# A bidirectional SSD scan with its step sizes moved into the exponent, and low weight parts made by DMA from an earlier point on

## The chip, the cores and the metric

One core of one Trainium2 chip runs the whole program. The engines named below are TensorE (PE in the profile, PEld for its weight loads), VectorE (DVE), ScalarE (ACT), GpSimd (POOL) and SyncE (SP, which issues most loads). The metric is the device time of one execution in microseconds, the median of several runs.

## The reference

One encoder layer runs on two independent sequences, a prompt of 512 tokens and a sample of 1024, with the same float32 weights. What matters here:

```python
u = group_rmsnorm(h, norm_mix_pre)
proj = u @ w_in                       # z, x/B/C, dt, and three hyena streams
# SSD: chunks of 128 tokens, 16 heads in 2 groups, forward and backward
a = dt * a_h;  a_cs = jnp.cumsum(a, axis=2)
decay_ts = jnp.exp(jnp.where(causal, seg, -jnp.inf))     # seg = a_cs[t] - a_cs[s]
scores = jnp.einsum('bctgn,bcsgn->bcgts', cr, br)
y_diag = jnp.einsum('bcgrts,bcsgrp->bctgrp', scores[:, :, :, None] * decay_ts, x * dt)
y_ssd = y_fwd + y_bwd + xs * ssd_d    # then gate with silu(z) and group norm
# hyena: short convolutions, then a long convolution by FFT
mix = concat([y_ssd, y_hy]) @ w_out   # residual, SwiGLU FFN, gated embedding
```

Inside a chunk, each pair of tokens (t, s) gets the score C_t.B_s times a decay of head and direction times the step size dt_s. On the diagonal both directions contribute with decay 1.

## The kernel before, in words

Matrix products keep nearly full float32 accuracy by splitting each operand into a high part (rounded to the fp32r format) and a low part (what the rounding lost), and running three matmuls: high x high (L301), low x high (L302), high x low (L303). A streamed weight half-tile of 128x512 is loaded by SyncE into `wst`. ScalarE then writes the high part `whi` (L292), and GpSimd subtracts it from the weight to get the low part `wlo` (L293). That is `split_w`. In `split_dma` ScalarE writes minus the rounded weight into `wlo` (L284), a DMA issued by GpSimd adds the weight to it (L285), and ScalarE writes `whi` in a second pass (L286). The flag `self.dma_lo` chooses between them in `load_w`. Six buffers of each of `wst`, `whi` and `wlo` run ahead of TensorE.

`build` calls the stages in this order: projections of the prompt, filters, scan of the prompt (`ssd(P)`), hyena projections and long convolution of the prompt; then for the sample the z and x/B/C projections, `ssd(S)`, `project_hy(S)` (the second convolution projections), `longconv(S)`; then the prompt's output projection, embedding projection and FFN, and the sample's. The order of the code isn't the order of execution: the Tile framework schedules all instructions with a timeline of its own and writes one in-order queue per engine, so a stage that keeps VectorE busy has large matrix products of a later stage between its instructions on TensorE. In the schedule before, `project_hy(S)` accompanies the prompt's long convolution and the start of the sample's scan, the prompt's output and embedding projections accompany the rest of that scan, and the prompt's FFN accompanies the sample's long convolution.

The scan handles one chunk c and one group g (8 heads) at a time: 8 units for the prompt, 16 for the sample, three pipeline stages. `stage_a` loads the cumulative decays of both directions, broadcast over the partitions, into `rw`, and computes the scores (L607), masked for the two directions into `su` and `sl` (L609, L610). For each head VectorE takes the smaller of the two directions' exponents (L615) and ScalarE the exponential (L617); that is E. Also for each head, ScalarE scales `sl` with the backward dt (L618) and VectorE adds `su` times the forward dt (L619); that is W. One VectorE product per unit multiplies W into E (L621). `stage_b` multiplies by x on TensorE (L628), adds D times x (GpSimd, L631) and the contributions of the carried states (L645, L646), and gates with z (L647). `stage_c` transposes and stores. Once per group a backward pass over all chunks (L590 to L597) prepares the backward states.

After the output projection of the prompt has been added up (L1108), `post_steps` scales, adds the residual and normalises four tiles of 128 tokens (L1059, L1060, L333), transposes them and splits them (L326). Only then can the prompt's FFN start.

## Time and profile before

| | before |
|---|---|
| median of 3 runs | 2855.22 us (2851.17 to 2855.67) |
| profiled execution: time | 2852.23 us |
| its span | 2850.3 us |
| TensorE / VectorE / ScalarE / GpSimd busy | 94% / 61% / 47% / 48% |
| scan of the prompt | about 480 to 640 us |
| scan of the sample | about 895 to 1235 us |
| long convolution of the sample | about 1250 to 1650 us |

An engine's busy share is a mean over stages with different limits. What a change is worth has to be read in the stage it lies in, from what TensorE waits for there. A group's row gives the line, engine, operation, tiles (written<-read), shape and count, then busy us and mean ns, then the idle time just before those instructions and what ended it.

### The profile page before, as it was taken

The numbers are of one execution on the slowest core, as the hardware profiler recorded it, in microseconds if no ns is written. First come the engines' busy times: TensorE is split into PE (matmuls) and PEld (weight loads), VectorE is DVE, ScalarE is ACT, GpSimd is POOL, SyncE is SP. The second block draws the span as 40 slices with busy tenths as digits, with TensorE's granted clock in tenths as the row PEclk, the third lists the DMA queues.
The fourth block names the chain that finished last, engine by engine and source line by source line (L and its number), as shares of the span: only waits on it lengthen the run. The fifth ranks groups of instructions, "written<-read, shape, count | busy, mean of one in ns | idle before, by whom it ended". The sixth has DMA issues, their size and how long they took to land.

```text
span 2850.3 us, 41685 instructions
## 1 busy us (share of the span) xinstructions
PE 2683.8 (94%) x14696; PEld 2254.9 (79%) x14696; DVE 1742.6 (61%) x2893; ACT 1336.4 (47%) x2580; POOL 1380.7 (48%) x1137
## 2 busy tenths in 40 slices
PE   7999999999999989889999998987799999999998
PEld 5987888778888767578778776766699999877776
DVE  6767896977666896966676734475343444325345
ACT  4434445773234564745444454365533333344453
POOL 4445555443453556535444444554454444445464
PEclk9999999999999999989999999999999999999999
DMA  5544555744345576778888886565632222366665
GB/s 169 180 137 127 150 174 185 219 141 138 99 123 160 154 249 202 223 206 206 199 181 204 187 218 218 177 222 183 157 100 82 79 75 86 119 207 207 203 202 186
DMA packets 448507, 480.04 MB, mean 168 GB/s; under 512 B 29409, under 2 KB 330281, under 8 KB 445995
## 3 DMA queue, kind: packets, MB, share of 16 engines
q1 hardware_dynamic: 340923, 347.34, 40.0%
q0 software_dynamic: 28224, 68.17, 10.8%
q10 hardware_dynamic: 79152, 61.88, 6.9%
q8 instruction: 116, 1.90, 0.3%
q14 instruction: 92, 0.75, 0.1%
HBM read 346.54 MB, written 91.95 MB: 154 GB/s over the span
## 4 chain that ended last, share of the span: by engine, by line
PE 66%; DVE 15%; DMA 8%; issue 5%; POOL 3%; ACT 2%; SPq 0%; POOLq 0%; ACTq 0%; DVEq 0%
PE g L301 17%; PE g L303 16%; PE g L302 16%; PE a L302 3%; PE a L303 3%; PE a L301 3%; PE a L700 1%; DVE b L692 1%; DVE W L619 1%; DVE E L615 1%; PE a L973 1%; POOL wlo L293 1%; DMA wlo<-wst 1%; PE a L404 1%; DMA mx<-mix_s 1%
## 5 line engine op out<-in xcount | busy, mean ns | idle before, releaser
L293 POOL TENSOR_TENSOR wlo<-wst,whi 128x512 fp32r<-128x512 f32 (+1 forms) x544 | 786.1, 1452 | 756.6 <-ACT whi L292 691.5
L292 ACT ACTIVATE whi<-wst 128x512 fp32r<-128x512 f32 (+1 forms) x544 | 339.5, 628 | 532.9 <-PE g L302 330.0
L301 PE MATMUL g<-uh,whi 128*128 128x512 f32 (+1 forms) x1232 | 493.5, 401 | 8.5 <-DVE cv L393 4.4
L303 PE MATMUL g<-uh,wlo 128*128 128x512 f32 (+1 forms) x1232 | 491.6, 399 | 0.0
L302 PE MATMUL g<-ul,whi 128*128 128x512 f32 (+1 forms) x1232 | 490.9, 398 | 0.0
L301 PE MATMUL g<-bh,whi 128*128 128x256 f32 x1056 | 293.0, 283 | 14.3 <-ACT sc L1266 3.8
L303 PE MATMUL g<-bh,wlo 128*128 128x256 f32 x1056 | 294.0, 281 | 4.2 <-DMA wlo<-mx 2.7
L302 PE MATMUL g<-bl,whi 128*128 128x256 f32 x1056 | 294.3, 280 | 0.0
L301 PEld LDWEIGHTS g<-uh,whi 128*128 128x128 f32 x1232 | 233.2, 189 | 67.5 <-issue 10.4
L303 PEld LDWEIGHTS g<-uh,wlo 128*128 128x128 f32 x1232 | 232.6, 189 | 53.9 <-issue 5.8
L302 PEld LDWEIGHTS g<-ul,whi 128*128 128x128 f32 x1232 | 232.9, 189 | 53.4 <-issue 7.2
L326 DVE TENSOR_TENSOR ml<-mx,mh 128x512 fp32r<-128x512 f32 x152 | 122.4, 808 | 222.0 <-ACT mh L325 221.9
L285 POOL DMA_DIRECT2D wlo<-wst x144 | 126.0, 930 | 226.2 <-ACT wlo L284 211.1
L393 DVE SCALAR_TENSOR_TENSOR cv<-g,cols,cv 128x510 f32<-128x510 f32 (+3 forms) x192 | 193.0, 1006 | 64.9 <-ACT cv L387 62.8
L301 PEld LDWEIGHTS g<-bh,whi 128*128 128x128 f32 x1056 | 197.2, 189 | 20.0 <-DVE gt L1227 6.1
L303 PEld LDWEIGHTS g<-bh,wlo 128*128 128x128 f32 x1056 | 199.6, 189 | 4.9 <-DMA wlo<-mx 2.9
L302 PEld LDWEIGHTS g<-bl,whi 128*128 128x128 f32 x1056 | 199.5, 189 | 0.1
L301 PE MATMUL g<-whi,mh 128*128 128x512 f32 x412 | 169.7, 412 | 23.7 <-ACT mh L325 16.3
L302 PE MATMUL g<-wlo,uh 128*128 128x264 f32 (+1 forms) x576 | 191.3, 332 | 0.5 <-POOL wlo L293 0.5
L303 PE MATMUL g<-whi,ul 128*128 128x264 f32 (+1 forms) x576 | 189.9, 331 | 1.6 <-DVE rs_t L308 1.6
L309 POOL TENSOR_TENSOR rs_t<-rs_t,nhalf 128x1 f32<-128x1 f32 (+2 forms) x112 | 120.0, 1074 | 144.0 <-DVE rs_t L308 141.5
L301 PE MATMUL g<-whi,uh 128*128 128x264 f32 (+1 forms) x576 | 189.0, 330 | 0.0
(334 smaller groups left out, 6030.5 us busy)
## 6 DMA issues: line engine op xcount, KB each, us to landing
wst<-in_w_in SPq DMA_DIRECT2D x192, 256.0 KB
wlo<-wst POOLq DMA_DIRECT2D x144, 256.0 KB, 4.9
wst<-in_w_down SPq DMA_DIRECT2D x132, 256.0 KB
wst<-in_w_out SPq DMA_DIRECT2D x96, 256.0 KB
wst<-in_w_gate SPq DMA_DIRECT2D x92, 256.0 KB
wst<-in_w_up SPq DMA_DIRECT2D x92, 256.0 KB
mx<-hid_s SPq DMA_DIRECT2D x88, 256.0 KB
rw<-rows_s SPq DMA_DIRECT2D x32, 512.0 KB
```

The source lines that it names most:

```text
L285: nc.gpsimd.dma_start(lo, w, accum_op=ALU.add)
L292: nc.scalar.activation(hi, w, AF.Copy)
L293: (eng or nc.gpsimd).tensor_tensor(out=lo, in0=w, in1=hi.bitcast(F32), op=ALU.subtract)
L301: nc.tensor.matmul(ps, lh, rh, start=first, stop=False, skip_group_check=shared)
L302: nc.tensor.matmul(ps, lh, rl, start=False, stop=False, skip_group_check=shared)
L303: nc.tensor.matmul(ps, ll, rh, start=False, stop=last, skip_group_check=shared)
L309: nc.gpsimd.tensor_tensor(out=t[:, :w], in0=t[:, :w], in1=self.nhalf[:, :w], op=ALU.pow)
L326: self.nc.vector.tensor_tensor(out=lo, in0=ps, in1=hi.bitcast(F32), op=ALU.subtract)
L393: nc.vector.scalar_tensor_tensor(out[:, a:b], ps[:, a + d:b + d], wcol(w), out[:, a:b], ALU.mult, ALU.add)
L404: nc.tensor.transpose(ps[:, j * 128:(j + 1) * 128], srcs[i + j], self.ident)
L615: nc.vector.scalar_tensor_tensor(E[:, h], rw[:, 0, h], dbf[:, c, gh:gh + 1], rw[:, 1, h], ALU.add, ALU.min)
L619: nc.vector.scalar_tensor_tensor(W[:, h], su, dt[:, c, gh:gh + 1], W[:, h], ALU.mult, ALU.add)
```

## The change: what it does

In the scan the step size dt goes into the exponent as its logarithm. `ssd_prep` computes log(max(dt, 1e-37)) - a_cs for all heads and both directions. `nb` becomes the backward part of it, and `dbf` the difference of forward and backward. E is then the decay times dt in one exponential, so the per-head W falls away (8 ScalarE and 8 VectorE instructions per unit), and all eight heads are multiplied with the unmasked scores in one product, as a broadcast. The masks move to the row tiles: two GpSimd `affine_select` instructions per unit set the excluded entries of `rw` to 1e30, so that the minimum picks the other direction. The forward direction keeps the diagonal. The backward direction's diagonal, score(t,t) times backward dt, is added to D: VectorE multiplies the scores with the identity, sums over the row and forms `cdd` for the eight heads, which takes the place of D in the GpSimd product with x. The scores are copied to SBUF by ScalarE. `rw` becomes two separate tiles from a ring of three, where before it was one double tile without a second buffer.

Apart from that, `dma_lo` is set before `project_hy(S)` and no longer before the prompt's FFN, so 84 more low parts are made by `split_dma`: 48 of `project_hy(S)`, 32 of the prompt's output projection and 4 of its embedding projection.

```diff
@@ ssd_prep
         dbf, nb = self.T(kp, [128, C, 16], "dbf"), self.T(kp, [128, C, 16], "nb")
-        nc.vector.tensor_tensor(out=dbf, in0=acs[:, :, 16:32], in1=acs[:, :, 0:16], op=ALU.subtract)
-        nc.vector.tensor_scalar(nb, acs[:, :, 16:32], -1.0, None, ALU.mult)
+        nc.vector.tensor_scalar(u, dt, 1e-37, None, ALU.max)
+        nc.scalar.activation(u, u, AF.Ln)
+        nc.vector.tensor_tensor(out=u, in0=u, in1=acs, op=ALU.subtract)
+        nc.vector.tensor_tensor(out=dbf, in0=u[:, :, 0:16], in1=u[:, :, 16:32], op=ALU.subtract)
+        nc.vector.tensor_copy(nb, u[:, :, 16:32])
@@ ssd_main, stage_a
-                rw = self.T(sp, [128, 2, 8, 128], "rw")
+                rw = [self.T(sp, [128, 8, 128], "rw", bufs=3) for _ in range(2)]
                 for d in range(2):
                     nc.sync.dma_start(
-                        rw[:, d], q.rows[d, c:c + 1, g * 8:(g + 1) * 8, :].to_broadcast([128, 8, 128]))
+                        rw[d], q.rows[d, c:c + 1, g * 8:(g + 1) * 8, :].to_broadcast([128, 8, 128]))
                 xt, zt, bk, bt, ct = load(c, g, ("x", "z", "bk", "bt", "ct"))
                 ps = self.aps()
                 nc.tensor.matmul(ps[:, 0:128], bt, ct, start=True, stop=True)
-                su, sl = self.T(sp, [128, 128], "su", bufs=2), self.T(sp, [128, 128], "sl", bufs=2)
-                nc.vector.tensor_tensor(out=su, in0=ps[:, 0:128], in1=self.tri[:, 0, :], op=ALU.mult)
-                nc.vector.tensor_tensor(out=sl, in0=ps[:, 0:128], in1=self.tri[:, 1, :], op=ALU.mult)
+                cb, dg = self.T(sp, [128, 128], "su", bufs=2), self.T(sp, [128, 128], "sl", bufs=2)
+                nc.scalar.activation(cb, ps[:, 0:128], AF.Copy)
+                nc.vector.tensor_tensor(out=dg, in0=ps[:, 0:128], in1=self.ident, op=ALU.mult)
+                cd, dd = self.T(sp, [128, 1], "cd", bufs=2), self.T(sp, [128, 8], "cdd", bufs=3)
+                nc.vector.tensor_reduce(cd, dg, mybir.AxisListType.X, ALU.add)
+                hs = slice(g * 8, (g + 1) * 8)
+                nc.vector.scalar_tensor_tensor(dd, dt[:, c, 16 + g * 8:24 + g * 8], cd, self.r_D[:, hs],
+                                               ALU.mult, ALU.add)
+                big = [[0, 8], [1, 128]], [[0, 8], [-1, 128]]
+                for d in range(2):
+                    nc.gpsimd.affine_select(out=rw[d], in_=rw[d], compare_op=(ALU.is_ge, ALU.is_gt)[d],
+                                            fill=1e30, base=0, pattern=big[d], channel_multiplier=(-1, 1)[d])
                 E = self.T(sp, [128, 8, 128], "E", bufs=2)
-                W = self.T(sp, [128, 8, 128], "W")
                 for h in range(8):
                     gh = g * 8 + h
-                    nc.vector.scalar_tensor_tensor(E[:, h], rw[:, 0, h], dbf[:, c, gh:gh + 1],
-                                                   rw[:, 1, h], ALU.add, ALU.min)
+                    nc.vector.scalar_tensor_tensor(E[:, h], rw[0][:, h], dbf[:, c, gh:gh + 1],
+                                                   rw[1][:, h], ALU.add, ALU.min)
                     nc.scalar.activation(E[:, h], E[:, h], AF.Exp, bias=nb[:, c, gh:gh + 1])
-                    nc.scalar.activation(W[:, h], sl, AF.Copy, scale=dt[:, c, 16 + gh:17 + gh])
-                    nc.vector.scalar_tensor_tensor(W[:, h], su, dt[:, c, gh:gh + 1], W[:, h],
-                                                   ALU.mult, ALU.add)
-                nc.vector.tensor_tensor(out=E, in0=W, in1=E, op=ALU.mult)
-                return xt, zt, bk, ct, E
+                nc.vector.tensor_tensor(out=E, in0=E, in1=cb.rearrange("p (o t) -> p o t", o=1).to_broadcast(
+                    [128, 8, 128]), op=ALU.mult)
+                return xt, zt, bk, ct, E, dd
@@ stage_b
-                nc.gpsimd.tensor_tensor(out=h3(y), in0=h3(xt),
-                                        in1=hb(self.r_D[:, g * 8:(g + 1) * 8]), op=ALU.mult)
+                nc.gpsimd.tensor_tensor(out=h3(y), in0=h3(xt), in1=hb(dd), op=ALU.mult)
@@ build
             self.stream("m")
+            self.dma_lo = True
             self.project_hy(S, pj, us)
...
-                self.dma_lo = True
                 u, chain = self.ffn(P, 0, pl, u)
                 self.dma_lo = False
```

The schedule moves with it. On VectorE, where the norm chain of the prompt's output projection meets the last units of the sample's scan, the queue before reads from the first row scaling (L1059) on as follows. Here `acc`, `t` and `rs_t` belong to the chain, all other tiles to the scan.

```order
L1059 SCALAR_TENSOR_TENSOR acc_12614<-acc_12614,rs_t_13279,row_13268 128x1024
L645 TENSOR_TENSOR yo_9509<-a_9507,ea_8044 128x512
L609 TENSOR_TENSOR su_9546<-a_9544,tri_7985 128x128
L610 TENSOR_TENSOR sl_9547<-a_9544,tri_7985 128x128
L1059 SCALAR_TENSOR_TENSOR acc_12616<-acc_12616,rs_t_13285,row_13268 128x1024
L1060 TENSOR_TENSOR t_2592_13272<-acc_12614,t_2592_13272 128x1024
L308 TENSOR_SCALAR rs_t_13291<-ss_13288 128x1
L646 TENSOR_TENSOR y_9492<-y_9492,yo_9509 128x512
L308 TENSOR_SCALAR rs_t_13297<-ss_13294 128x1
L1060 TENSOR_TENSOR t_2593_13274<-acc_12616,t_2593_13274 128x1024
L619 SCALAR_TENSOR_TENSOR W_9551<-su_9546,dt_8015,W_9551 128x128 x3
L633 TENSOR_TENSOR y_9594<-y_9594,a_9585 128x512
```

After it (ten lines are added ahead, so L1059, L1060 and L1108 are now L1069, L1070 and L1118) the same place reads:

```order
L1069 SCALAR_TENSOR_TENSOR acc_12526<-acc_12526,rs_t_13227,row_13210 128x1024
L1070 TENSOR_TENSOR t_2640_13214<-acc_12524,t_2640_13214 128x1024
L655 TENSOR_TENSOR yo_9479<-a_9477,ea_7999 128x512
L1118 TENSOR_TENSOR acc_12525<-acc_12525,g_13049 128x512
L1118 TENSOR_TENSOR acc_12527<-acc_12527,g_13049 128x512
L1070 TENSOR_TENSOR t_2641_13216<-acc_12526,t_2641_13216 128x1024
L656 TENSOR_TENSOR y_9462<-y_9462,yo_9479 128x512
L615 TENSOR_TENSOR sl_9518<-a_9515,ident_105 128x128
L631 TENSOR_TENSOR E_9531<-E_9531,su_9517 128x1024
L308 TENSOR_SCALAR rs_t_13233<-ss_13230 128x1
L643 TENSOR_TENSOR y_9558<-y_9558,a_9549 128x512
L600 TENSOR_TENSOR pf_9561<-pf_9561,a_9564 128x512
```

The W rows are gone, and the last piece of the output projection (L1118) now stands one scan unit later relative to the scan. From it to the last low part of the FFN's input (L326) the scan has 14 rows left, and the E rows of the last unit (L628) stand ahead of it.

On GpSimd, between units of the sample's scan, the queue before reads as follows (`xw` is the state's input, `y` the unit's output, `wlo` a low weight part):

```order
L590 TENSOR_TENSOR xw_8839<-lx_8673,wd_8046 128x512
L293 TENSOR_TENSOR wlo_12665<-wst_12662,whi_12664 128x512
L631 TENSOR_TENSOR y_8733<-lx_8571,r_D_7993 128x512
L647 TENSOR_TENSOR y_8631<-y_8631,lz_8471 128x512
L309 TENSOR_TENSOR rs_t_8655<-rs_t_8655,nhalf_110 128x1
L590 TENSOR_TENSOR xw_9021<-xw_9021,wd_8046 128x512
L293 TENSOR_TENSOR wlo_12695<-wst_12692,whi_12694 128x512
L631 TENSOR_TENSOR y_8835<-lx_8673,r_D_7993 128x512
```

And in the changed kernel:

```order
L593 TENSOR_TENSOR xw_8653<-lx_8500,wd_8001 128x512
L623 AFFINE_SELECT rw_8593<-rw_8593 128x1024
L657 TENSOR_TENSOR y_8457<-y_8457,lz_8310 128x512
L642 TENSOR_TENSOR y_8553<-lx_8404,cdd_8421 128x512
L623 AFFINE_SELECT rw_8688<-rw_8688 128x1024
L309 TENSOR_TENSOR rs_t_8481<-rs_t_8481,nhalf_110 128x1
L285 DMA wlo_12571<-wst_12568 128x512
L593 TENSOR_TENSOR xw_8749<-lx_8596,wd_8001 128x512
L623 AFFINE_SELECT rw_8689<-rw_8689 128x1024
L285 DMA wlo_12578<-wst_12575 128x512
```

Two selects per unit have come in, apart from each other, and the subtractions have become DMA issues.

2 lines of the change are left out of this document (1 added, 1 removed).

## The prediction

> **What bounds the kernel now.** I read the busy shares first, then the busy time by stage, then the idle time ahead of single instructions, and last the groups on the engines that the change touches. The whole execution:
>
> ```profile
> span 2850.3 us, 41685 instructions
> PE 2683.8 (94%) x14696; PEld 2254.9 (79%) x14696; DVE 1742.6 (61%) x2893; ACT 1336.4 (47%) x2580; POOL 1380.7 (48%) x1137
> ```
>
> TensorE is busy for 94% of the span, so work taken from another engine is worth only what TensorE waits for that engine. By stage (columns: window, length, then busy us and count of PE, PEld, DVE, ACT, POOL; granted clock; DMA share; GB/s):
>
> ```profile
> 640.00:895.00 255.00, 255.00 (x1308) 214.72 (x1307) 165.82 (x228) 84.63 (x117) 107.02 (x74) 1.00 0.40 114
> 500.00:525.00 25.00, 22.44 (x101) 16.89 (x100) 20.63 (x37) 16.24 (x33) 10.45 (x8) 1.00 0.67 206
> 525.00:550.00 25.00, 23.81 (x119) 17.60 (x118) 23.96 (x50) 18.92 (x46) 10.46 (x9) 1.00 0.77 238
> 895.00:1232.00 337.00, 309.76 (x1389) 235.26 (x1388) 275.43 (x504) 198.08 (x502) 186.66 (x145) 0.95 0.68 211
> 960.00:1025.00 65.00, 64.81 (x319) 50.40 (x318) 61.81 (x132) 42.04 (x118) 35.41 (x25) 1.00 0.64 196
> 1025.00:1050.00 25.00, 17.98 (x61) 12.24 (x60) 23.07 (x41) 14.72 (x38) 14.49 (x9) 0.80 0.77 263
> 1112.00:1150.00 38.00, 38.00 (x187) 29.71 (x186) 33.91 (x67) 23.15 (x69) 22.98 (x19) 1.00 0.63 201
> 1150.00:1232.00 82.00, 61.98 (x252) 43.77 (x251) 70.05 (x131) 54.39 (x137) 44.06 (x42) 0.84 0.71 213
> 1250.00:1650.00 400.00, 379.82 (x1885) 315.39 (x1885) 271.42 (x446) 178.56 (x302) 182.67 (x142) 0.98 0.85 196
> ```
>
> From 640 to 895 us TensorE has no gap at all. The sample's scan lies in 895 to 1232. There VectorE is busy for 275.4 of 337 us, and TensorE, which fills the stage with the convolution and output projections, lacks 27.2 us. Almost all of it is in two places: 7.0 us at 1025 to 1050 and 20.0 us at 1150 to 1232. In the same two places the granted clock is 0.80 and 0.84. As an estimate from these rows, 17.98 busy us at 0.80 hold 3.6 us that full clock would not need, and 61.98 at 0.84 hold 9.9. **The most that a faster scan can give in this stage is 27.2 + 13.5 = 40.7 us.** Who is waited for there:
>
> ```profile
> 1031.12 3.44 PE L628 MATMUL a<-lx,E 128*128 128x64 f32 x16 [3.24 <-DVE yo L645]
> 1172.74 0.68 DVE L1108 TENSOR_TENSOR acc<-acc,g 128x512 f32<-128x512 f32 x1
> 1179.85 1.27 DVE L1108 TENSOR_TENSOR acc<-acc,g 128x512 f32<-128x512 f32 x2
> 1228.57 0.38 PE L301 MATMUL g<-uh,whi 128*128 128x256 f32 x1 [1.22 <-ACT uh L325]
> 1181.10:1228.60 47.50, 41.24 (x76) 0.78 0.87 259
> ```
>
> At 1031 TensorE stands at the scan's y product until VectorE has read an accumulator. At 1181.1 VectorE has added the last piece of the prompt's output projection (L1108), and the prompt's FFN starts 47.5 us later, at 1228.6. The last row is VectorE's busy time in between (41.2 us of 47.5, 76 operations): the norm chain of four token tiles, interleaved on VectorE's in-order queue with the last scan steps.
>
> **The change, part by part.** VectorE in the sample's scan, the engine waited for:
>
> ```profile
> L619 DVE SCALAR_TENSOR_TENSOR W<-su,dt,W 128x128 f32<-128x128 f32 x128 | 61.9, 534 | 5.9 <-ACT W L618 5.7
> L615 DVE SCALAR_TENSOR_TENSOR E<-rw,dbf 128x128 f32<-128x128 f32 x128 | 42.5, 389 | 3.9 <-DMA rw<-rows_s 3.9
> L621 DVE TENSOR_TENSOR E<-W,E 128x1024 f32<-128x1024 f32 x16 | 21.2, 1323 | 0.1
> L609 DVE TENSOR_TENSOR su<-a,tri 128x128 f32<-128x128 f32 x16 | 4.5, 280 | 0.4 <-PE a L607 0.4
> L980 DVE TENSOR_REDUCE hss<-b 128x8 f32<-128x512 f32 (+1 forms) x16 | 15.2, 952 | 16.1 <-ACT b L978 16.0
> L308 DVE TENSOR_SCALAR rs_t<-ss 128x1 f32<-128x1 f32 x96 | 13.5, 145 | 49.1 <-ACT junk L316 49.1
> ```
>
> Removed: 61.9 (W) + 2 x 4.5 (the masks, L609 and its twin L610) = 70.9 us. Added per step: the diagonal product, like L609, 0.28; the row sum over 128 columns, between 0.15 (L308) and 0.95 (L980), taken as 0.35 since it reads a quarter of L980's columns or less; the small cdd operation, about L308's 0.15. Sixteen steps make 12.5 us. E and the product E times scores keep their size. VectorE loses 58 of 275 us, or 3.6 us per step.
>
> ScalarE loses 128 scalings and gains a copy of the scores per step (0.30, as `ch`) and one more pass per low part:
>
> ```profile
> L618 ACT ACTIVATE W<-sl,dt 128x128 f32<-128x128 f32 x128 | 39.5, 394 | 16.4 <-DVE sl L610 14.5 <-DVE E L621 1.3 <-ACT mt L659 0.4
> L918 ACT ACTIVATE ch<-a 128x128 f32<-128x128 f32 x32 | 9.5, 296 | 0.0
> L284 ACT ACTIVATE wlo<-wst 128x512 fp32r<-128x512 f32 x144 | 89.0, 619 | 57.8 <-PE g L302 49.8 <-DMA wst<-in_w_down 7.7
> L617 ACT ACT_TABLE_LOAD x7 | 9.0, 1283 | 0.1
> ```
>
> The 48 low parts made between 895 and 1232 all switch (row L293 below): -39.5 + 4.7 + 29.7 = -5 us on an engine that is 59% busy. Four more table loads (28 before, 32 now) come with the logarithm, 1.28 us each. They lie in the preparation at 890 and 470, beside full TensorE windows, and cost nothing unless TensorE has run dry.
>
> GpSimd gets two selects per step and gives up the subtractions:
>
> ```profile
> L293 POOL TENSOR_TENSOR wlo<-wst,whi 128x512 fp32r<-128x512 f32 x48 | 72.7, 1523 | 25.9 <-ACT whi L292 25.9
> L285 POOL DMA_DIRECT2D wlo<-wst x144 | 126.0, 930 | 226.2 <-ACT wlo L284 211.1 <-issue 4.9 <-PE g L302 4.4
> masks.py:199 POOL TENSOR_SCALAR_AFFINE_SELECT ident<-ident 128x128 f32<-128x128 f32 x1 | 0.3, 282 | 0.0
> L1511 POOL MEMSET const-float32-0.0<- 128x1 f32 x1 | 0.1, 98 | 0.2 <-issue 0.2
> L819 POOL TENSOR_SCALAR w<-w 64x1024 f32<-64x1024 f32 x1 | 2.8, 2787 | 0.1
> ```
>
> The trace has one select, 128x128 in 0.28 us. With a start of 0.10 (the 1-column memset) the rest is 1.44 ns a column, so 1024 columns take 1.6 us. The upper bound is L819, 2.8 us for a one-input operation of 1024 columns. I take 1.6, being the same operation. GpSimd: 32 x 1.6 = 51, less 48 x (1.52 - 0.93) = 28, so 187 becomes 210 of 337 us (238 at the upper bound).
>
> The added transfers: 84 low parts of 256 KB.
>
> ```profile
> q0 software_dynamic: 28224, 68.17, 10.8%
> wlo<-wst POOLq DMA_DIRECT2D x144, 256.0 KB, 4.9
> ```
>
> That queue takes 10.8% of 2850 us for 68.17 MB, 4.5 us per MB, so 1.2 us of all engines for one part: 57 us for the 48 in the stage, which lifts its DMA share from 0.68 to 0.85. The prompt's FFN runs at 0.85 (1250 to 1650) with TensorE 95% busy, so I charge little. The other 36 fall between 640 and 895, at share 0.40 beside a full TensorE: nothing either way.
>
> Interference is the part with no row of its own. VectorE's two-input operations stretch beside GpSimd's:
>
> ```profile
> L619 DVE SCALAR_TENSOR_TENSOR W<-su,dt,W x192: 335/343/2393, 498.9 to 1212.3; 128x128 f32<-128x128 f32 x192
> L645 DVE TENSOR_TENSOR yo<-a,ea x40: 669/682/693, 529.9 to 1224.5; 128x512 f32<-128x512 f32 x40
> ```
>
> L619, with two operands in SBUF, goes from a median of 0.34 up to 2.39 us; L645, with one in PSUM, never moves. Bounds for the net effect: the 28 us taken off GpSimd's subtractions give VectorE some back, 51 us of selects may take more; I put it at zero, with 8 us to either side. The Trainium skill, "GPSIMD Engine Reference", section 1 Specifications, says that GpSimd's SBUF interfaces are shared with VectorE and contend with VectorE instructions that have two SBUF inputs. By it the selects, which run just ahead of the two-input E operations, would take about 5 us of the VectorE saving; the L619 row agrees with the rule for two-input GpSimd work, and no row here shows a select beside VectorE.
>
> **The sum**, against the profiled execution's own 2852.2 us (span 2850.3 and 1.9 around it):
> - 1025 to 1050: 7.0 idle and 3.6 of clock. Two steps' saving (7.2 us) covers the wait. I take two thirds: -7.
> - 1150 to 1232: in the 47.5 us between the last L1108 and the FFN's start the chain's own operations are these:
>
> ```profile
> L1059 DVE SCALAR_TENSOR_TENSOR acc<-acc,rs_t,row 128x1024 f32<-128x1024 f32 x4 | 6.6, 1650 | 0.0
> L333 DVE SCALAR_TENSOR_TENSOR acc<-t,rs_t,row 128x1024 f32<-128x1024 f32 x4 | 5.0, 1276 | 0.0
> L1060 DVE TENSOR_TENSOR t<-acc,t 128x1024 f32<-128x1024 f32 x4 | 4.9, 1217 | 2.4 <-DMA t<-in_x_prompt 2.4
> ```
>
> These 16.5 us, with 5 for the small scalings and low parts, leave about 20 of the 41.2 to the scan: two steps' W, a step's E, two products, and the accumulators. In the changed order, from the last such addition to the last low part of the FFN's input, the scan has 14 operations there: one product (1.2), a mask, a row sum and cdd (0.8 together) and ten accumulator operations of 0.7 (as L645), 9 us. That is 11 us less ahead of the FFN: -11. Matmuls of the step that moved ahead are paid in a window that has its own gap (the 7 above), and that is why I don't take more.
> - The prompt's scan at 500 to 550: 3.8 us idle, half recovered: -2.
> - 895 to 1025 and 1050 to 1150: TensorE full, nothing.
> - The selects ahead of E, low parts that land 4.9 us after issue, the table loads: +3.
>
> Sum -17: **2835 us**. The three runs shown have a median of 2855.2, 3 us above the profiled one, which this sum does not move for. After 1250 TensorE is 95% busy with the same work, so what is won is kept.
>
> **Rivals.**
> - *The gap only moves.* The norm chain also waits for other things: its reload of the residual (`t<-in_x_prompt`, for which the L1060 row above shows 2.4 us of idle VectorE) and GpSimd's root, now behind selects. If these end last, the 1150 gap stays. What is left is a few us: 2852. For it: GpSimd's queue is in order. Against: VectorE is 85% busy in that window.
> - *GpSimd's selects become the scan's pace (slower).*
>
> ```profile
> 960.00:1072.00 112.00, 9.71 (x8) 0.95 0.72 227
> 495.30 5.88 DMA rw<-rows_p
> ```
>
> The first row counts the scan's products (L621) in 112 us: 8, so a step every 14 us; the second is a row load that E stood waiting for. One of the two row tiles of a step can only be loaded once E of the step before is done; then come the load, GpSimd's queue, the select, and E. E at 8 x 0.34 = 2.7, the load 5.9, a turn in the queue of 3 (two operations like L293) and 1.6 make 13.2; from a select of about 2.3 us upward the loop exceeds 14. At 2.8 us and doubled queueing it is 17, and 14 steps x 3 us, half covered by filler matmuls, gives +20: 2872. The Trainium skill, "GPSIMD Engine Reference", section 4.1 Engine selection, advises against elementwise work on GpSimd because it is about twice as slow as VectorE; that favours this rival.
> - *The low parts arrive late (slower).* Share 0.85 delays weights and scan loads alike; if each of the 36 tiles of the prompt's output and embedding projections waits 0.3 us more, that is +11, less a few us won: 2860.
> - *All of the ceiling.* Both gaps close and the clock stays up: 2852 - 41 = 2811.
>
> **How the numbers follow.** Forecast (2825 to 2846) 0.55; all of the ceiling 0.11; the gap moves 0.17; selects set the pace 0.12; late low parts 0.05. A change of under 0.2% (5.7 us) can't be told from none here. Faster: 0.55 + 0.11 = 0.66, and the moved gap is the same: 0.17; slower 0.17. The range leaves out the tails of the ceiling and of the slow cases: 2813 to 2863.
>
> **What would show it.** VectorE's busy time between scan start and FFN start falls by 50 to 65 us; no operation on W is left; the FFN's first matmul comes 30 to 40 us after the last L1108 counterpart; clock at both places back to 0.9 or more. Wrong if a select takes over 2.3 us, if E waits mainly for GpSimd, or if the FFN's start still trails by 45 us.

## The result, and the profile after

The change made the kernel slower: 2891.6 us (median of 5 runs, 2881.7 to 2894.8) against 2854.4 (5 runs, 2851.2 to 2855.7), a ratio of 1.0121 with a 95% interval of [1.0104, 1.0137], or about 35 us. I had forecast 2835, and 0.17 for slower. Below, differences "in us" are ratios times 2855, since each group of runs has its own runs of the kernel before.

The page of the change begins like this, and its row of the software queue follows:

```profile
span 2893.0 us, 41630 instructions
PE 2695.0 (93%) x14696; PEld 2263.3 (78%) x14696; DVE 1669.5 (58%) x2729; ACT 1332.4 (46%) x2502; POOL 1378.6 (48%) x1185
q0 software_dynamic: 40320, 90.20, 15.0%
```

VectorE did lose work, 73 us over the whole execution, and yet TensorE's busy share fell from 94% to 93%. Where it fell, the windows tell (columns as in the prediction: length, busy us of PE, PEld, DVE, ACT, POOL, granted clock, DMA share, GB/s). The kernel before in the sample's scan and the turn to the long convolution:

```profile
895.00:1300.00 405.00, 375.38 (x1767) 292.15 (x1766) 316.01 (x576) 231.43 (x563) 211.16 (x167) 0.95 0.71 212
```

The change in the window before it, in the same window, and up to the start of the prompt's FFN:

```profile
640.00:895.00 255.00, 255.00 (x1308) 214.75 (x1307) 150.06 (x230) 105.06 (x156) 89.16 (x75) 1.00 0.62 150
895.00:1300.00 405.00, 345.31 (x1605) 265.06 (x1604) 235.62 (x414) 203.03 (x467) 190.95 (x184) 0.93 0.83 228
895.00:1256.00 361.00, 312.09 (x1390) 234.91 (x1388) 223.44 (x391) 186.73 (x438) 185.01 (x177) 0.94 0.83 229
```

From 895 to 1300 us TensorE's idle time doubled, from 30 to 60 us, while the DMA share rose from 0.71 to 0.83. On either side TensorE is as busy as it was (255.00 us in 640 to 895, and 380.29 in 1300 to 1700 where it was 380.06). Most of the added idle time, 17.7 us, lies between 1050 and 1150 us, where the kernel before had no gap; before, then the change:

```profile
1050.00:1150.00 100.00, 100.00 (x470) 78.09 (x469) 75.14 (x131) 58.28 (x148) 62.91 (x48) 1.00 0.68 218
1050.00:1150.00 100.00, 82.35 (x345) 62.28 (x346) 44.59 (x73) 50.58 (x110) 45.88 (x42) 0.88 0.87 249
```

The first matmul of the long convolution dates the loss; before, and then in the change, with the FFN's first matmul and the additions to which it is tied:

```profile
1248.81 0.94 PE L700 MATMUL a<-b,fw 128*128 128x128 f32 x7
```

```profile
1221.68 1.27 DVE L1118 TENSOR_TENSOR acc<-acc,g 128x512 f32<-128x512 f32 x2
1255.88 0.38 PE L301 MATMUL g<-uh,whi 128*128 128x256 f32 x1 [0.70 <-ACT uh L325]
1284.58 1.19 PE L710 MATMUL a<-b,fw 128*128 128x128 f32 x4 [9.67 <-issue]
```

It starts 35.8 us later. The FFN follows the last addition by 32.9 us where it was 47.5, but that addition itself comes 41.8 us later. The two executions differ by 42.7 us in all, so most of the loss has arisen by 1285 us. Who waits for whom on GpSimd between 890 and 1260 us (sum, times, longest, in us), first before, then in the change:

```profile
POOL xw L590 <- DMA lx<-xs_s: 20.9, 8, 3.6
POOL xw L590 <- DMA xw<-xs_s: 19.3, 9, 4.3
```

```profile
POOL rw L623 <- DMA rw<-rows_s: 37.5, 14, 7.5
POOL xw L593 <- DMA xw<-xs_s: 35.1, 8, 9.1
POOL xw L593 <- DMA lx<-xs_s: 25.5, 8, 6.8
```

Two things stand out: the selects (L623) wait for the row loads at the head of GpSimd's queue, and its waits for the states' inputs (`xw`, `lx`) have grown from 40.2 to 60.6 us.

### The profile page after: what moved, and what is told of

It is laid out like the page before. It is cut to its first block, busy times and chain, and to the rows that moved or that the text cites. A ratio compares the mean times of both kernels' runs of the same rounds, so it can differ in the third digit from the quotient of the medians.

```text
span 2893.0 us, 41630 instructions
## 1 busy us (share of the span) xinstructions
PE 2695.0 (93%) x14696; PEld 2263.3 (78%) x14696; DVE 1669.5 (58%) x2729; ACT 1332.4 (46%) x2502; POOL 1378.6 (48%) x1185
## 4 chain that ended last, share of the span: by engine, by line
PE 64%; DMA 11%; DVE 10%; issue 7%; POOL 4%; ACT 3%; SPq 1%; POOLq 0%; ACTq 0%; DVEq 0%
PE g L301 16%; PE g L303 16%; PE g L302 16%; PE a L301 3%; PE a L303 3%; PE a L302 3%; DMA wlo<-wst 2%; PE a L710 2%; DMA rw<-rows_s 1%; PE a L983 1%; POOL wlo L293 1%; DVE b L702 1%; PE a L404 1%; POOL rs_t L309 1%; DMA lbk<-bk_s 1%
## 5 line engine op out<-in xcount | busy, mean ns | idle before, releaser
L293 POOL TENSOR_TENSOR wlo<-wst,whi 128x512 fp32r<-128x512 f32 (+1 forms) x460 | 663.7, 1450 | 636.0 <-ACT whi L292 593.7
L292 ACT ACTIVATE whi<-wst 128x512 fp32r<-128x512 f32 (+1 forms) x460 | 287.6, 629 | 424.8 <-PE g L302 256.3
L285 POOL DMA_DIRECT2D wlo<-wst x228 | 200.7, 928 | 357.6 <-ACT wlo L284 310.1
L326 DVE TENSOR_TENSOR ml<-mx,mh 128x512 fp32r<-128x512 f32 x152 | 120.9, 798 | 220.2 <-ACT mh L325 218.3
L286 ACT ACTIVATE whi<-wst 128x512 fp32r<-128x512 f32 x228 | 142.7, 626 | 216.3 <-PE g L302 158.2
L301 PE MATMUL g<-whi,uh 128*128 128x264 f32 (+1 forms) x576 | 194.9, 339 | 6.1 <-ACT uh L325 5.1
L301 PE MATMUL g<-whi,mh 128*128 128x512 f32 x412 | 171.6, 416 | 20.6 <-ACT mh L325 14.4
```

The source lines that it names most:

```text
L285: nc.gpsimd.dma_start(lo, w, accum_op=ALU.add)
L286: nc.scalar.activation(hi, w, AF.Copy)
L292: nc.scalar.activation(hi, w, AF.Copy)
L293: (eng or nc.gpsimd).tensor_tensor(out=lo, in0=w, in1=hi.bitcast(F32), op=ALU.subtract)
L301: nc.tensor.matmul(ps, lh, rh, start=first, stop=False, skip_group_check=shared)
L326: self.nc.vector.tensor_tensor(out=lo, in0=ps, in1=hi.bitcast(F32), op=ALU.subtract)
```

## The experiments

All stand beside runs of the kernel before on the same chip, so rows are compared by their ratios and not by their medians. "First E" (its start), "last E" (its end) and "long convolution" (the start of its first matmul) are times in us of one profiled execution each.

| kernel | median us | ratio to before, 95% | first E | last E | long convolution |
|---|---|---|---|---|---|
| before | 2854.4 | 1 | 902 | 1199 | 1249 |
| the change | 2891.6 | 1.0121 [1.0104, 1.0137] | 906 | 1215 | 1285 |
| scan's change only | 2863.3 | 1.0017 [0.9997, 1.0037] | 905 | 1189 | 1250 |
| early low parts by DMA only | 2878.4 | 1.0081 [1.0064, 1.0098] | 905 | 1216 | 1276 |
| both, DMA only for convolution projections | 2864.7 | 1.0031 [1.0017, 1.0046] | 909 | 1200 | 1266 |
| both, DMA only from output projection on | 2872.0 | 1.0059 [1.0043, 1.0075] | 906 | 1202 | 1263 |
| before + 84 unused transfers | 2894.5 | 1.0149 [1.0127, 1.0171] | 903 | 1231 | 1289 |
| before + two ScalarE passes, sum on GpSimd | 2856.3 | 1.0015 [0.9999, 1.0030] | 905 | 1198 | 1254 |
| before, FFN's low parts on GpSimd too | 2914.5 | 1.0195 [1.0173, 1.0217] | 907 | 1208 | 1260 |
| scan's change, FFN's low parts on GpSimd too | 2913.9 | 1.0197 [1.0173, 1.0222] | 906 | 1190 | 1252 |
| scan's change, y*z on VectorE | 2852.8 | 1.0003 [0.9990, 1.0016] | 907 | 1188 | 1252 |
| scan's change, no selects | 2850.1 | 0.9994 [0.9985, 1.0004] | 896 | 1177 | 1241 |
| the same, one double row tile | 2832.9 | 0.9924 [0.9908, 0.9941] | 895 | 1162 | 1228 |
| scan's change, no diagonal part | 2862.0 | 1.0027 [1.0011, 1.0043] | 910 | 1209 | 1267 |
| before without W | 2833.1 | 0.9914 [0.9896, 0.9933] | 895 | 1161 | 1230 |
| before without W, broadcast product | 2843.9 | 0.9956 [0.9937, 0.9975] | 897 | 1168 | 1230 |
| before without W, + selects | 2860.5 | 1.0025 [1.0013, 1.0037] | 906 | 1191 | 1255 |
| before without W, + selects on a dead tile | 2840.4 | 0.9953 [0.9938, 0.9968] | 901 | 1177 | 1241 |
| scan's change, four row tiles | 2857.1 | 1.0012 [1.0000, 1.0023] | 901 | 1197 | 1248 |
| scan's change, masks on VectorE | 2876.7 | 1.0079 [1.0064, 1.0094] | 909 | 1223 | 1276 |

### The two parts apart

The scan's change with the flag where it was:

```diff
-            self.dma_lo = True
             self.project_hy(S, pj, us)
...
+                self.dma_lo = True
                 u, chain = self.ffn(P, 0, pl, u)
```

> The scan's change alone; the low parts go by DMA from FFN P on, as in the kernel before. Theory Q (in the change GpSimd's selects stand in its one queue behind the row loads, and y*z, rstd and the state products behind them come late): the loss is the scan's own, so this kernel is as slow as the change, 2880 to 2895 us, and the distance from the first E to the first product of the sample's long convolution stays near the change's 384 us (before: 349). Theory D (the added low-part transfers crowd the DMA engines while the scan loads its tiles): without them the scan's saving of 58 us of VectorE shows, 2825 to 2845 us, and that distance falls below 345 us.

The flag's move with the old scan, on the kernel before:

```diff
+            self.dma_lo = True
             self.project_hy(S, pj, us)
...
-                self.dma_lo = True
                 u, chain = self.ffn(P, 0, pl, u)
```

> The kernel before with the low parts by DMA from the second convolution projections on; the scan is the old one. Theory Q: GpSimd is relieved of 84 subtractions, 2835 to 2856 us, no slower than before. Theory D: the scan's loads wait as in the change, 2880 to 2910 us, with the DMA share of the stretch 895 to 1300 us at 0.80 or more (before: 0.71).

And the change with the flag set for one part of the early projections only, off again before the output projection (first diff), or set only from there (second):

```diff
             self.dma_lo = True
             self.project_hy(S, pj, us)
+            self.dma_lo = False
...
+                self.dma_lo = True
                 u, chain = self.ffn(P, 0, pl, u)
```

```diff
-            self.dma_lo = True
             self.project_hy(S, pj, us)
+            self.dma_lo = True
```

> The change with the low parts by DMA only for the second convolution projections and again from FFN P on; output projection P and the embedding projection split on GpSimd as before. Theory Q: 2880 to 2895 us. Theory D: the convolution projections run at 640 to 973 us and mostly ahead of the sample's scan, so this is near the kernel with the scan's change alone, 2830 to 2850 us; if the transfers at the scan's start (900 to 973 us) are the ones that hurt, it stays at 2865 or more.

> The change with the low parts by DMA from output projection P on, the second convolution projections split on GpSimd as before. Theory Q: 2880 to 2895 us. Theory D: the transfers that lie in the scan are these, so it keeps most of the loss, 2870 to 2890 us.

Both theories were half right. The early transfers alone cost 23 us, the scan's change alone nothing that can be told from zero, and together they cost 35. That is 7 more than the sum, which the three intervals, of about 5 us to either side each, do not tell from none. With the scan's change already in, the convolution projections' part adds 4 us and the output projection's part 12, yet both together add 30. These 14 us more are just clear of the intervals, and they are not explained here.

Where the 23 us come from shows in the group change of the sample's scan, where a backward pass over all chunks must be done before the next E. Two units' E run ahead of it, so the gap lies between the tenth and the eleventh unit: before, their first E operations are 55 us apart, with the early transfers alone 72, and in the change 68. So 17 of the 28 us by which the early transfers alone delay the long convolution arise there. SyncE's queue of the kernel before in that place (start, us of the row, then the load; a row of several loads holds their waits too):

```profile
1075.02 0.43 SPq L589 DMA_DIRECT2D xw<-xs_s  x1
1076.87 4.76 SPq L277 DMA_DIRECT2D wst<-in_w_out  x2
1081.73 0.37 SPq L579 DMA_DIRECT2D lbk<-bk_s  x1
1082.16 0.42 SPq L589 DMA_DIRECT2D xw<-xs_s  x1
```

The same place with the early transfers alone:

```profile
1084.48 0.42 SPq L589 DMA_DIRECT2D xw<-xs_s  x1
1085.00 10.26 SPq L277 DMA_DIRECT2D wst<-in_w_out  x4
1095.36 0.39 SPq L579 DMA_DIRECT2D lbk<-bk_s  x1
1095.84 0.39 SPq L589 DMA_DIRECT2D xw<-xs_s  x1
1096.64 6.47 SPq L277 DMA_DIRECT2D wst<-in_w_out  x2
...
1104.71 0.38 SPq L589 DMA_DIRECT2D xw<-xs_s  x1
```

What SyncE waited for with its weight loads (L277) between 890 and 1260 us, in the kernel before:

```profile
SPq L277 <- POOL wlo L293: 67.8, 38, 5.0
SPq L277 <- DMA wlo<-wst: 32.5, 8, 10.8
```

With the early transfers alone, the same, and the waits of GpSimd and TensorE for the scan's loads:

```profile
SPq L277 <- DMA wlo<-wst: 136.1, 42, 8.2
POOL xw L590 <- DMA lx<-xs_s: 48.3, 9, 8.2
POOL xw L590 <- DMA xw<-xs_s: 33.2, 10, 8.1
PE a L592 <- DMA lbk<-bk_s: 8.0, 2, 4.6
```

And TensorE's longest wait in the change:

```profile
PE a L595 <- DMA lbk<-bk_s: 12.8, 4, 6.1
```

The loads of `xw` are issued 11.4 and 8.9 us apart, where it was 7.1. Ahead of each stands a weight load that waits for a free `wst`, and a `wst` is now free only when the low part's transfer has landed; these waits of SyncE rose from 100.3 to 136.1 us. SyncE issues in order, so the scan's loads wait behind the weights. GpSimd's waits for `lx` and `xw` doubled, from 40.2 to 81.5 us. TensorE itself, which in the kernel before waits for no transfer in this stretch, now waits for the scan's loads (`lbk`), and in neither kernel for a weight.

### The transfer, or ScalarE's second pass

On the kernel before, each of the 84 weight tiles gets one more transfer of the same size, which nobody reads; and in the other kernel ScalarE makes its two passes, but GpSimd makes the sum:

```diff
             hi, lo = self.split_dma(st) if self.dma_lo else self.split_w(st)
+            if self.extra:
+                nc.gpsimd.dma_start(st, hi.bitcast(F32), accum_op=ALU.add)
```

```diff
         nc.scalar.activation(lo, w, AF.Copy, scale=-1.0)
-        nc.gpsimd.dma_start(lo, w, accum_op=ALU.add)
+        if self.two_pass:
+            nc.gpsimd.tensor_tensor(out=lo, in0=lo.bitcast(F32), in1=w, op=ALU.add)
+        else:
+            nc.gpsimd.dma_start(lo, w, accum_op=ALU.add)
```

> The kernel before, with every low part still subtracted on GpSimd, and from the second convolution projections to the embedding projection 84 further DMAs of 256 KB, each adding the high part to the weight tile that is no longer read; only the reuse of that buffer waits for it. Theory C (the added transfers themselves crowd the scan's loads): it loses what the kernel with the early low parts by DMA alone loses, 15 to 30 us, 2870 to 2887; xw and lx waits of GpSimd in 890 to 1260 us rise from 40 to 70 us or more. Theory A (it is ScalarE's second pass, or that the low part lands late for TensorE): within 6 us of before.

> The kernel before, with ScalarE's two passes for the same 84 low parts, but the sum of weight and negated high part made by GpSimd and not by DMA. Theory A: ScalarE's 84 x 0.62 us of second passes cost most of the 23 us: 2868 to 2885. Theory C: no added transfer, within 6 us of before.

The unused transfers cost 43 us, the second passes 4, which the interval does not tell from none. So transfers that nobody reads are enough for such a loss, and ScalarE's passes are not needed. Whether a low part that lands late would cost something by itself, no run shows. But the wait that I had named did not rise: GpSimd's waits for `xw` and `lx` are 35.6 us here. What shows instead is the buffer, and GpSimd's cost of issuing (these rows are of the kernel with the unused transfers, 890 to 1260 us):

```profile
SPq L279 <- DMA wst<-whi: 104.9, 35, 6.3
L273 POOL DMA_DIRECT2D wst<-whi x48 | 44.2, 984 | 4.9 <-POOL wlo L295 4.2 <-DMA wst<-in_w_in 0.3 <-DMA xw<-xs_s 0.3
```

Three things come with such a transfer: the engines' time, the longer hold on `wst` with SyncE's queue behind it, and 0.98 us of GpSimd. No run separates them. More `wst` buffers would, and that was not tried.

If transfers cost so much, are they also wrong beside the long convolution, where the kernel before has them? Two kernels drop the line that sets the flag before the FFN, from the kernel before and from the one with the scan's change only:

```diff
-                self.dma_lo = True
                 u, chain = self.ffn(P, 0, pl, u)
```

> The kernel before with no early low parts by DMA at all: the 144 of the prompt's FFN, beside the long convolution, are subtracted on GpSimd too (and those of the last stages, where the flag was off, as they were). Theory C (a 256 KB accumulating transfer costs about 0.3 to 0.5 us of the end time wherever the DMA share is over 0.7): the stage from 1300 to 1700 falls from share 0.84 to about 0.6 and the time by 10 to 40 us. If GpSimd's 86 us more of work in that stage hold up the convolution's products instead, 2860 to 2890.

> The scan's change with no low parts by DMA ahead of the last stages. Theory C: 10 to 40 us under the scan's change alone (2863). If GpSimd is the bound without them: 2865 to 2900.

Each comes out 56 us above the kernel before, the second 51 above the scan's change alone. So the first theory, a price per transfer wherever the DMA share is high, falls. From 1300 to 1700 us, the kernel before, and then without these transfers:

```profile
1300.00:1700.00 400.00, 380.06 (x1846) 313.72 (x1846) 247.88 (x398) 182.67 (x306) 178.91 (x142) 0.98 0.84 198
```

```profile
1300.00:1700.00 400.00, 338.40 (x1603) 280.54 (x1603) 306.02 (x387) 107.17 (x166) 227.73 (x128) 0.92 0.36 110
```

The DMA share falls from 0.84 to 0.36 and TensorE loses 42 us there, since GpSimd's subtractions come in, VectorE stretches from 248 to 306 busy us, and the convolution's products wait (33.6 us for VectorE's `b`). The same transfer pays beside one stage and costs beside another, and the DMA share (0.84 there, 0.83 in the change's scan) does not tell which.

### What the scan's change could have given

Three kernels ask whether VectorE was the wrong engine. The scan's change without selects; with the gate product on VectorE; and the kernel before with W taken out:

```diff
-                for d in range(2):
-                    nc.gpsimd.affine_select(out=rw[d], in_=rw[d], ...
```

```diff
-                nc.gpsimd.tensor_tensor(out=y, in0=y, in1=zt, op=ALU.mult)
+                nc.vector.tensor_tensor(out=y, in0=y, in1=zt, op=ALU.mult)
```

```diff
-                    nc.scalar.activation(W[:, h], sl, AF.Copy, scale=dt[:, c, 16 + gh:17 + gh])
-                    nc.vector.scalar_tensor_tensor(W[:, h], su, dt[:, c, gh:gh + 1], W[:, h],
-                                                   ALU.mult, ALU.add)
-                nc.vector.tensor_tensor(out=E, in0=W, in1=E, op=ALU.mult)
```

> The scan's change alone, low parts as before, and the two selects per unit left out, so the minimum is taken over unmasked rows and y is not the reference's. It takes 35 us (32 x 1.1) out of GpSimd's queue in the sample's scan, and the waits for row loads that stood in it. Theory G (the selects in GpSimd's in-order queue hold up y*z, the root and the states behind them, and eat what VectorE saves): at least 10 us faster than with them, 2835 to 2850 us against 2863, and ScalarE's wait for y*z ahead of the sum of squares falls from 50 us to under 25. Theory T (the scan's pace does not matter, the end of the stage is set by TensorE's order and the chain behind the prompt's output projection): within 5 us of the kernel with selects, 2858 to 2868.

> The scan's change alone, low parts as before, with the gate product y*z on VectorE, which has the time to spare, where it stood on GpSimd behind the selects. Theory G: y*z no longer waits behind row loads and selects; ScalarE's wait ahead of the sum of squares falls from 50 us to under 25, and the time by 8 to 20 us, 2843 to 2855. Theory T: 2858 to 2868.

> The kernel before with W left out (no scaling of sl, no addition of su times dt, no product with E; M is the bare exponential, so y is not the reference's) and nothing put in its place. It takes 128 x (0.53 + 0.39) us and 16 products of 1.3 us, 83 us of VectorE and 40 of ScalarE, out of the sample's scan, more than the change does, and touches neither GpSimd nor the transfers. Theory V (VectorE is what TensorE waits for in that stage, as the prediction had it): 2815 to 2838 us. Theory B (the end of the stage is set by the transfers of the turn from scan to long convolution and by the chain behind the output projection, and what TensorE gets earlier it gives back later): 2840 to 2858.

Without W the kernel gains 25 us, so VectorE's work in the scans is worth something: 83 us taken away in the sample's scan and 30 in the prompt's gave 25, or 0.2 us per us. (59 us of ScalarE's scalings went with them.) 5 of the 25 us have arisen by 895 us: up to there TensorE is idle for 28 us, where it was 33.

The scan's change alone does not take 58 us off VectorE. Up to the FFN's start it takes 34 (274.4 to 240.3), and without its selects 42, and it gives nothing that can be told from zero in either. The rest goes into longer operations: with the selects, E takes 52.0 us between 890 and 1260 where it took 42.5, the product 28.4 where it took 21.2, and `cdd` 0.64 us a piece where 0.15 was forecast.

Moving y*z to VectorE is worth 4 us (1.0017 to 1.0003), which is inside the intervals. GpSimd's delayed queue shows in ScalarE's wait for y*z; with the selects, then without:

```profile
ACT junk L316 <- POOL y L657: 49.8, 15, 7.5
ACT junk L316 <- POOL y L654: 14.0, 13, 3.0
```

This wait falls by 36 us and the time by 7, so most of it does not reach the end.

Four more kernels go from the one end to the other. To the kernel without W come the broadcast product with E, or the selects; from the scan's change the diagonal's operations are left out; and in the kernel without selects only the row tiles go back:

```diff
+                nc.vector.tensor_tensor(out=E, in0=E, in1=su.rearrange("p (o t) -> p o t", o=1).to_broadcast(
+                    [128, 8, 128]), op=ALU.mult)
```

```diff
+                for d in range(2):
+                    nc.gpsimd.affine_select(out=rw[:, d], in_=rw[:, d], ...
```

```diff
-                nc.vector.tensor_tensor(out=dg, in0=ps[:, 0:128], in1=self.ident, op=ALU.mult)
-                nc.vector.tensor_reduce(cd, dg, mybir.AxisListType.X, ALU.add)
-                nc.vector.scalar_tensor_tensor(dd, dt[:, c, 16 + g * 8:24 + g * 8], cd, self.r_D[:, hs],
-                                               ALU.mult, ALU.add)
+                dd = self.r_D[:, g * 8:(g + 1) * 8]
```

```diff
-                rw = [self.T(sp, [128, 8, 128], "rw", bufs=3) for _ in range(2)]
+                rw = self.T(sp, [128, 2, 8, 128], "rw")
```

> The kernel before without W, but with the change's one product of E with masked scores (a broadcast over eight heads): y is not the reference's. VectorE loses 62 us and ScalarE 40, nothing is added. Theory V (the gain goes with VectorE's busy time, 22.6 us for 83): 0.27 x 62 = 17 us, 2834 to 2843. Theory L (the product stands between the last exponential and the y products of TensorE, and it is this delay that counts): the gain is gone, 2848 to 2858.

> The kernel before without W and its product, plus only the change's two selects per unit on GpSimd (y is not the reference's). Theory G (the selects, each waiting in GpSimd's queue for a row load, cost 6 to 12 us in whatever kernel): 2838 to 2846, against 2833 without them. If they are free where the scan has slack: 2831 to 2836. Theory O (the order of the queues, which the schedule sets anew for each kernel, makes the difference between the kernels): anything from 2833 to 2860, and the scan units that stand behind the last L1108 addition tell it.

> The scan's change alone, low parts as before, without the diagonal's operations (no product with the identity, no row sum, no cdd; D as before, so y lacks the backward direction on the diagonal). Theory V: VectorE loses 12 us more, worth 3 us: 2857 to 2862. Theory L: GpSimd's product D times x no longer waits for VectorE's row sum and the PSUM buffer of the scores comes free earlier, 2845 to 2856.

> The scan's change without selects, and with the row loads into one double tile as before in place of the ring of three (y is not the reference's). Theory R (two tiles out of a ring of three let the second row load of a unit start only when the unit before has read its first, and that sets the pace): 2835 to 2843, against 2850 with the ring. Theory V and O: 2846 to 2853, the ring makes no difference.

The last one gains 22 us. It has no masks, so it shows what the rest is worth. **The logarithm and the product of eight heads do give about the forecast gain; the kernels with the masks on GpSimd and with the new row tiles lose it again.** The selects, put into the kernel without W, cost 32 us (0.9914 to 1.0025). The ring of three row tiles costs 20 us where there are no selects (0.9924 to 0.9994). The two do not add: on the ring the selects cost only 7 (0.9994 to 1.0017). The diagonal's operations cost nothing that can be told from zero. The broadcast product's run lies between both theories, with single times from 2829 to 2854, and decides nothing.

How the ring costs 20 us is only half seen. E waits as long for row loads in both kernels; the ring first, then the double tile:

```profile
L625 DVE SCALAR_TENSOR_TENSOR E<-rw,dbf,rw 128x128 f32<-128x128 f32 x128 | 44.4, 413 | 8.8 <-DMA rw<-rows_s 8.8
```

```profile
L625 DVE SCALAR_TENSOR_TENSOR E<-rw,dbf 128x128 f32<-128x128 f32 x128 | 39.3, 374 | 10.0 <-DMA rw<-rows_s 10.0
```

The scan is 14 us longer with the ring (first E to last E 281 against 267 us). 6.5 of these arise just ahead of the tenth unit's E and 5.8 just ahead of the last one's. In both places VectorE's queue has more work of the prompt's output projection ahead of E than with the double tile. For the tenth unit it is two more splits of its input (L326), which wait 4.6 us for ScalarE; for the last it is the first steps of the norm chain for two of its four tiles (L1066, L1067). One row of each:

```profile
1043.45 1.47 DVE L326 TENSOR_TENSOR ul<-t,uh 128x1024 fp32r<-128x1024 f32 x1 [3.77 <-ACT uh L325]
1166.17 2.29 DVE L1067 TENSOR_TENSOR t<-acc,t 128x1024 f32<-128x1024 f32 x1
```

So 12 of the 14 us arise where the order on VectorE's queue differs, which the schedule sets anew for each kernel. Behind the last addition of the output projection one scan unit is left with the ring and none without. Whether the ring brings this order about, or any other edit of this size would, stays open.

### Why the selects cost so much

The selects of the change's size, in the kernel without W, on a tile that nobody loads or reads; the scan's change with a fourth row tile, for which one of the six weight buffers had to go; and the masks as one VectorE addition, with the double row tile:

```diff
+                    nc.gpsimd.affine_select(out=dead, in_=dead, compare_op=(ALU.is_ge, ALU.is_gt)[d],
```

```diff
-                rw = [self.T(sp, [128, 8, 128], "rw", bufs=3) for _ in range(2)]
+                rw = [self.T(sp, [128, 8, 128], "rw", bufs=4) for _ in range(2)]
```

```diff
-                    nc.gpsimd.affine_select(out=rw[d], in_=rw[d], ...
+                nc.vector.tensor_tensor(out=rw, in0=rw, in1=far.rearrange(
+                    "p d (o t) -> p d o t", o=1).to_broadcast([128, 2, 8, 128]), op=ALU.add)
```

> The kernel before without W and its product, plus two selects per unit of the change's size on a tile that is neither loaded nor read. GpSimd does the same work as with the selects on the row tiles, but no select waits for a load and no E waits for a select. Theory H (head of line: the wait for the row load stops the whole GpSimd queue, and E waits behind it): 2833 to 2842, most of the 27 us is gone. Theory T (GpSimd's own time, 1.1 us a piece, or its share of the SBUF port beside VectorE): 2850 to 2860 remains.

> The scan's change alone, low parts as before, with a ring of four row tiles, so that both rows of a unit can be loaded while the unit before still reads its own (room for it is made by five in place of six buffers of the loaded weights and one of the diagonal product). Theory H: GpSimd's wait for row loads falls from 19.5 to under 8 us and the time to 2843 to 2855. Theory T: the loads were not the point, 2856 to 2868.

> The scan's change with one double row tile as before, the low parts as before, and the masks added on VectorE as 0 or 1e30 in one operation of 2048 columns per unit; no selects in the loop. It computes the reference's outputs. VectorE gets about 2.4 us a unit, 38 us, back, so 20 of the 58 us remain; at 0.27 us per us of VectorE (22.6 for 83): 5 us won, 2845 to 2852. If the masks' operation at the head of E delays each unit as the selects do: 2855 to 2870.

On the dead tile, where no select waits for a load and no E for a select, 11 of the 32 us are left (0.9914 to 0.9953). GpSimd's groups between 890 and 1260 us (busy us, mean ns, then its idle time just before), on the row tiles and on the dead tile:

```profile
L613 POOL TENSOR_SCALAR_AFFINE_SELECT rw<-rw 128x1024 f32<-128x1024 f32 x32 | 36.5, 1149 | 20.6 <-DMA rw<-rows_s 19.0 <-DMA lbt<-bt_s 0.7 <-DVE cv L393 0.6
```

```profile
L616 POOL TENSOR_SCALAR_AFFINE_SELECT dead<-dead 128x1024 f32<-128x1024 f32 x32 | 36.7, 1146 | 0.7
```

The work is the same, 36.6 us. On the row tiles GpSimd also stands still for 20.6 us, and with it everything queued behind: the state products, y*z, the roots, the low parts. But the wait is not all that differs. Nothing holds the dead selects back, and the schedule puts them early (min/median/max ns, then first and last start, in both scans):

```profile
L613 POOL TENSOR_SCALAR_AFFINE_SELECT rw<-rw x48: 1082/1092/1547, 491.5 to 1183.4; 128x1024 f32<-128x1024 f32 x48
L616 POOL TENSOR_SCALAR_AFFINE_SELECT dead<-dead x48: 1082/1092/1549, 483.0 to 972.2; 128x1024 f32<-128x1024 f32 x48
```

On the row tiles the sample's 32 selects lie between all of its units; on the dead tile they are done after the first three. So this kernel takes the wait away and also moves the work, and how much of the 21 us goes to each no run shows. In both, TensorE's idle time up to 895 us is already 33 us where it is 28 without selects. E's own row shows the other end, without selects, on the row tiles and on the dead tile:

```profile
L614 DVE SCALAR_TENSOR_TENSOR E<-rw,dbf 128x128 f32<-128x128 f32 x128 | 42.8, 405 | 11.4 <-DMA rw<-rows_s 11.4
```

```profile
L618 DVE SCALAR_TENSOR_TENSOR E<-rw,dbf 128x128 f32<-128x128 f32 x128 | 50.7, 465 | 15.7 <-POOL rw L613 15.7
```

```profile
L621 DVE SCALAR_TENSOR_TENSOR E<-rw,dbf 128x128 f32<-128x128 f32 x128 | 53.6, 489 | 12.1 <-DMA rw<-rows_s 12.1
```

Some of the 11 us of the dead tile is seen here too: E becomes 10.8 us longer, though it has nothing to do with these selects. This lies in the units that run beside them. The E of the first unit, and that of the fifth, after the last select:

```profile
900.62 7.88 DVE L621 SCALAR_TENSOR_TENSOR E<-rw,dbf 128x128 f32<-128x128 f32 x8 [7.41 <-DMA rw<-rows_s]
991.24 2.18 DVE L621 SCALAR_TENSOR_TENSOR E<-rw,dbf 128x128 f32<-128x128 f32 x8
```

One operation takes 1.17 us where a select alone runs beside it, and 0.34 with GpSimd idle. On the row tiles no operation of E runs beside a select; its 7.9 us more come with other GpSimd work, beside which 39 of the 128 run, and 19 without selects.

The fourth row tile did not help (1.0012, inside the interval of the ring of three), and GpSimd's wait for row loads stayed where it was (19.5 us with three):

```profile
POOL rw L623 <- DMA rw<-rows_s: 19.4, 12, 4.8
```

So one tile more, with one weight buffer less, does not shorten this wait. Loads that stand late in SyncE's queue would fit that, which no run shows. The masks on VectorE are worst, and above both ranges that I had given:

```profile
L628 DVE TENSOR_TENSOR rw<-rw,far 128x2048 f32<-128x2048 f32 x16 | 41.0, 2562 | 30.3 <-DMA rw<-rows_s 30.3
```

Now VectorE's in-order queue stands for 30.3 us at the row load, and each row tile is free 2.6 us later. The kernel without selects and with the same double tile is 44 us faster (0.9924 to 1.0079). The masks' 41 us of VectorE would be worth 9 at 0.2 us per us, so their work alone does not explain it; the wait, 10.0 us there and 30.3 here, fits, and is not shown to be all of the rest. Wherever the mask sits between the row load and E, the engine that carries it waits for the load. No kernel that keeps the masks was faster than the kernel before; the best, with y*z on VectorE, is level with it.

## Why the prediction was wrong, by its own steps

- **VectorE's 58 us, and the sum of -17.** Right in mechanism and about in size, but only without selects and with the old row tiles, where the change gives -22. In the change VectorE's busy time up to the FFN's start fell by 51 us (274.4 before in 895 to 1228, 223.4 in 895 to 1256), inside the forecast 50 to 65, and the FFN trails by 33 us, inside 30 to 40. Where GpSimd keeps its subtractions, as in the scan's change alone, it fell by only 34. The new operations were sized too small: `cdd`, taken as 0.15 us, took 0.39 to 0.69 in the four kernels compared, and the product, taken as unchanged at 21.2 us, took 24.8 to 28.4. And a shorter trail isn't an earlier start. The addition it is counted from moved behind the scan's last E (before, one unit's E rows stood behind it), and it is itself fed by the same stage.
- **"895 to 1025 and 1050 to 1150: TensorE full, nothing."** This step failed. In the change TensorE is idle there for 5.1 and 17.7 us, against 0.2 and none before. That is 22 of the 30 us that it lost between 895 and 1300. A window without a gap tells what cannot be won in it, not what can be lost, and the sum had no term for a loss there.
- **"The selects ahead of E, low parts that land 4.9 us after issue, the table loads: +3."** This step failed. The select's duration was forecast too high; the change's selects (min/median/max ns), and its E group in 890 to 1260 us:

```profile
L623 POOL TENSOR_SCALAR_AFFINE_SELECT rw<-rw x48: 1085/1096/2152, 489.1 to 1206.0; 128x1024 f32<-128x1024 f32 x48
L628 DVE SCALAR_TENSOR_TENSOR E<-rw,dbf,rw 128x128 f32<-128x128 f32 x128 | 40.7, 386 | 4.3 <-POOL rw L623 4.1
```

  1.10 us, not 1.6. So its duration was not what this step priced too low. I had added it to GpSimd's 187 us of 337 as busy time, on an engine with room, and had not priced what is queued behind a select that waits for a load. Measured: 32 us in the kernel without W, for 48 selects of about 55 us in all, and 7 us with the ring, in the scan's change. How much of the 32 is the wait and how much the work stays open. (The upper bound of GpSimd's busy time is a slip as well: 187 and 32 x 2.8 less 28 make 248, not 238. Nothing else rests on it.)
- **The ring of row tiles.** The sum has no term for it. Without selects it costs 20 us (0.9924 to 0.9994), and 12 of the 14 us by which the scan is longer lie where VectorE's queue has other work ahead of E.
- **"Interference zero, 8 us to either side."** For E in the change itself zero was right: 40.7 us, where it was 42.5. With GpSimd's subtractions kept beside the selects it is 52.0, so about 2 us of time at 0.2 us per us. The Trainium skill, "GPSIMD Engine Reference", section 1 Specifications, with its shared SBUF interfaces, had the sign right there, and the dead tile's rows agree with it also for a one-input GpSimd operation. Section 4.1 Engine selection of the same page of the Trainium skill, by which I favoured slow selects, excepts one-input operations as running near line rate; 1.10 us for 1024 columns agrees (VectorE's two-input addition of that size, L1060, took 1.22).
- **"It lifts its DMA share from 0.68 to 0.85 ... I charge little."** This step failed as well, for 23 us alone and 30 on top of the scan's change. The share came out as estimated (0.83). The comparison with the FFN's stage at 0.85 did not carry over. There, in 1300 to 1700 us before, no engine's waits for one kind of transfer sum to more than 7.7 us. The scan's backward pass is a chain of load, product, matmul and addition, for whose loads GpSimd already waited 40.2 us, and these loads stand behind the weights in SyncE's queue. "A DMA share that another stage stands" was the wrong measure.
- **"The other 36 fall between 640 and 895: nothing."** Right for that window: TensorE is busy for 255.00 of 255 us before and after.
- **"After 1250 what is won is kept."** Right to within 8 us: from the long convolution's first matmul to the last matmul it takes 1590 us before, and 1584 to 1598 in all kernels that make the FFN's low parts by DMA.
- **The rivals.** "Selects set the pace" was right in sign, and its +20 us lies between the 7 and the 32 measured. But its threshold (a select of 2.3 us or more) was not reached, and the cost came anyway; the rival counted one loop of E and not GpSimd's queue. "Low parts arrive late" had the right cause in the transfers, with too small a price, +11 against 23, and a chance of 0.05. It priced a wait of the weight tiles; in the runs TensorE waits for the scan's loads. Both happened at once, which none of my cases held.
- **"Wrong if a select takes over 2.3 us, if E waits mainly for GpSimd, or if the FFN's start still trails by 45 us."** The first and the last did not come true (1.10 us; 33 us), and the second only in share: of E's 4.3 us of waiting 4.1 were for GpSimd, too little to be the loss. The clock at 1025 to 1050 us rose from 0.80 to 0.92, as forecast, but between 1050 and 1150 it fell from 1.00 to 0.88. The signs watched VectorE and E, while the waits lay on GpSimd's and SyncE's queues.
